# Program order on VectorE, ScalarE and TensorE in parts of a decoder layer, and a second buffer for the weights' side sums

## The chip, the cores and the metric

The kernel runs on one core of a Trainium2 chip. The metric is the device time of one execution in microseconds (us). TensorE multiplies into PSUM; VectorE, ScalarE and GpSimd prepare its operands in SBUF and take its results out of PSUM (GpSimd works on SBUF only); SyncE issues the transfers. The views call these engines PE (PEld is its weight load), DVE, ACT, POOL and SP.

## What is computed

One decoder layer on 1024 tokens of width 1024, in fp32:

```python
x = LN(ALPHA * x + 0.5 * swiglu(x, ffn_w13[0], ffn_w2[0]))      # FFN a
x = LN(ALPHA * x + token_mixer(x))                              # retention and sparse attention
x = LN(ALPHA * x + 0.5 * swiglu(x, ffn_w13[1], ffn_w2[1]))      # FFN b
e = (p @ w_ple) * sigmoid(x @ w_ple_gate)                       # ple
x = LN(ALPHA * x + e)

swiglu(x, w13, w2) = (silu(a) * u) @ w2,   a, u = split(x @ w13)     # inner width 2816
token_mixer(x)     = concat(nsa(x), silu(g) * retention(q, k, v)) @ w_out
retention          : 4 heads of width 128, rotary q and k, chunks of 128 tokens with a decayed state
```

## The kernel before

An fp32 operand is held as two parts, hi and lo. ScalarE makes hi (a rounded copy, L104, L140 or L144), and VectorE or GpSimd makes lo = operand - hi (L105, L141 or L145). A product is three matmuls: hi x hi, lo x hi, hi x lo.

**FFN, first half (up).** It is computed in blocks with seven products in place of eight, by Strassen and Winograd. The 22 tiles of the inner width are numbered f. The first two use plain blocks; from the third tile (f = 2) on, `steps_up` lists (tile, product) steps in program order, 140 of them, and each step is 12 matmuls of 128x512. The operands of a step come from `items_up`: four raw weight blocks wr are loaded for a tile, and side sums of them (s1 to s4) are built by `mix` (L394). A `Stream` holds 8 operands ahead (tiles ch and cl). The results of a tile are put together in `after`: s on ScalarE (L465), t, r, s and h on VectorE (L471 to L482, from PSUM tile Y and the SBUF tile s). They have to be read before TensorE may use those PSUM banks again.

For each pair q of tiles there are two pieces of work in a queue `bg`, one entry of which is emitted after each step: the side sums hq of the result (`pair`, L493 to L502), which are stored to the DRAM tile hd, and the side sums of the second weight (`right_down`). The latter load 1 MB of w2 into the tile w2r, form three differences (L445 to L447) and a fourth (L442) on VectorE in place, and store the whole tile to the DRAM tile td. There is one w2r buffer. Emission is program order, but the order in which an engine runs its instructions is made by a scheduler that may move them; only GpSimd and the places under `self.order(engine)` keep program order.

**FFN, second half (down).** Seven products for each of 11 values of q, in groups of 3, 4 and 4 (`GROUPS`), again with 12 matmuls for each q, operands dr loaded from hd, td and w2. A product of a group is summed over its q in four PSUM banks, and `settle` then adds it to its homes: parts of acc in SBUF on VectorE (L607), or the extra tile u1, whose first use is a copy by ScalarE (L599). acc starts as the residual, 8 loads of 512 KB (L587). The order is `PRODUCTS`: product 0 has the homes c11 in acc and u1; product 5 has u1 alone.

**Retention.** Four heads. For a head, TensorE computes the projections pq and pk (each a PSUM pair of two banks); they are rotated: ScalarE copies halves into sw (L851, L852), and VectorE multiplies by cos straight from PSUM (L853) and adds sw x sin (L856, L857). `ret_head` makes the scores, the states and the output of a head; `weave` spreads these six steps, called side, between the matmuls of the next projection. The list hid, turn and finish is work of the attention's compressed keys that is put in the same gaps. The PSUM tag ps has two pairs. The next weights of a projection are split by ScalarE into wh (L144) when the matmuls that read the old ones are done. Behind the last head comes the projection pg of the gate.

**ple.** The input p is split into pH (ScalarE) and pL (GpSimd, through `split_sb`, L145); the embedding product pe waits for pH, pL and the split weights wh, wl.

Of the kernel before, what the change touches and what calls it, by code (L numbers as in the profile page):

```python
# [10 lines left out]
F32 = mybir.dt.float32  # L11
# [7 lines left out]
P = 128  # L19
# [10 lines left out]
HALF = 512  # L30
NP = NFF // 2
GROUPS = (3, 4, 4)
SLOTS = 8
PRODUCTS = (0, 1, 5, 4, 2, 6, 3)
UORD = [(i, g) for pair in ((4, 2), (5, 1), (6, 0), (3,), (7,)) for g in range(2) for i in pair]


# [86 lines left out]
class Layer:  # L124
# [252 lines left out]
    def items_up(self, j, steps):  # L377

        nc, A = self.nc, self.A
        raw, S = {}, {}  # L380
        left = dict.fromkeys(range(NFF), 0)

        def load(f):
            if f >= NFF or f in raw:
                return
            raw[f] = {}
            for a, b in ((0, 0), (0, 1), (1, 0), (1, 1)):
                t = raw[f][a, b] = self.wr.tile([P, HALF], F32, tag="wr", bufs=self.raws, name=self.nm("wr"))
                nc.sync.dma_start(t, A["w13"][j, f, a, b])

        def mix(name, f, x, y, op):
            e = nc.gpsimd
            t = S[name, f] = self.sm.tile([P, HALF], F32, tag=name, bufs=2 if name == "s2" else 1, name=self.nm(name))
            e.tensor_tensor(t, x, y, op)  # L394
            return t

        def sums(f):
            if (f, "s") not in S:
                S[f, "s"] = True
                r = raw[f]  # L400
                mix("s1", f, r[1, 0], r[1, 1], ALU.add)
                mix("s2", f, S["s1", f], r[0, 0], ALU.subtract)

        for f in (0, 1):
            for a, b in ((0, 0), (1, 0), (0, 1), (1, 1)):
                t = self.wr.tile([P, HALF], F32, tag="wr", bufs=self.raws, name=self.nm("wr"))
                nc.sync.dma_start(t, A["w13"][j, f, a, b])
                yield t, nc.vector
        load(2)
        e = nc.gpsimd  # L410
        for f, p in steps:
            r = raw[f]
            if p == 0:
                yield r[0, 0], e
            elif p == 1:
                yield r[0, 1], e
            elif p == 4:
                sums(f)
                yield S["s1", f], e
            elif p == 5:  # L420
                sums(f)
                yield S["s2", f], e
            elif p == 6:
                yield mix("s3", f, r[0, 0], r[1, 0], ALU.subtract), e
            elif p == 3:
                yield r[1, 1], e
            else:
                yield mix("s4", f, r[0, 1], S["s2", f], ALU.subtract), e
            left[f] += 1
            if left[f] == 3:  # L430
                load(f + 1)

    def right_down(self, j, q):

        nc = self.nc
        raw = self.ub.tile([P, 2, 2, HALF], F32, tag="w2r", bufs=1, name=self.nm("w2r"))
        nc.sync.dma_start(raw, self.A["w2"][j, q])
        b11, b12, b21, b22 = raw[:, 0, 0], raw[:, 0, 1], raw[:, 1, 0], raw[:, 1, 1]
        sub = ALU.subtract

        def final():
            nc.vector.tensor_tensor(b21, b21, b22, sub)  # L442
            nc.sync.dma_start(self.td[j][q], raw.rearrange("p a b n -> p (a b) n"))

        return [lambda: nc.vector.tensor_tensor(b11, b12, b11, sub),  # L445
                lambda: nc.vector.tensor_tensor(b12, b22, b12, sub),
                lambda: nc.vector.tensor_tensor(b22, b22, b11, sub), final]  # L447

    def ffn_up(self, j, B, hooks):

        nc = self.nc
        steps = self.steps_up()
        st = self.stream
        X, YZ, s, t, r, hs, W = {}, {}, {}, {}, {}, {}, {}
        add = ALU.add
        bg = deque()
# [57 lines left out]
        for half, right in enumerate(((B[0], B[1]), (B[6], B[2]))):  # L514
            for f in (0, 1):
# [12 lines left out]
                h = hs[f][:, half]  # L528
# [3 lines left out]
                    x()  # L532
        bg.extend(self.right_down(j, 0))
        pair(0, hs.pop(0), hs.pop(1))
        for f, p in steps:
            if p == 0:
                X[f] = self.one("X")
            if f not in YZ and p > 3:
                YZ[f] = self.two("Y")
            out = X[f] if p < 2 else YZ[f][:, 0] if p in (5, 6, 3) else YZ[f][:, 1]  # L540
            product(out, st.next(), B[p], p in (0, 5, 4), True)
            st.fill()
            after(f, p)
            if bg:
                bg.popleft()()
        while bg:
            bg.popleft()()

    def items_down(self, j):
        nc = self.nc  # L550
        q0 = 0
        todo = []
        for g in GROUPS:
            todo += [(q, p) for p in PRODUCTS for q in range(q0, q0 + g)]
            q0 += g
        srcs = []
        for q, p in todo:
            srcs.append(self.hd[j][q][:, p])
            srcs.append({0: self.A["w2"][j, q][:, 0, 0], 1: self.A["w2"][j, q][:, 1, 0],
                         2: self.A["w2"][j, q][:, 1, 1]}.get(p) if p < 3 else self.td[j][q][:, {3: 2, 4: 0, 5: 3, 6: 1}[p]])  # L560
        srcs = deque(srcs)
        raws = deque()

        def load():
            if srcs:
                t = self.wr.tile([P, HALF], F32, tag="wr", bufs=self.raws, name=self.nm("dr"))
                nc.sync.dma_start(t, srcs.popleft())
                raws.append(t)

        for _ in range(self.raws - 1):  # L570
            load()
        k, n = 0, len(srcs) + len(raws)
        while raws:
            load()
            k += 1
            yield raws.popleft(), nc.vector if k % 4 == 0 or k > n - 16 else nc.gpsimd

    def ffn_down(self, j, ln, residual, pool):

        nc = self.nc  # L580
# [30 lines left out]
        bg = deque()  # L611
        k = 0
        for g, n in enumerate(GROUPS):
            final = g == len(GROUPS) - 1
            for p in PRODUCTS:
                if k % 2 == 0:
                    pair = self.two("py"), self.two("py")
                    banks = [pair[m // 2][:, m % 2] for m in range(4)]
                else:
                    banks = [self.one("py"), self.one("py"), self.one("py"), self.lone("py")]  # L620
                k += 1
                for q in range(n):
                    (hh, hl), (wh, wl) = st.next(), st.next()
                    for m in range(4):
                        ms = slice(m * P, m * P + P)
                        nc.tensor.matmul(banks[m], hh[:, ms], wh, start=q == 0, stop=False)  # L626
                        nc.tensor.matmul(banks[m], hh[:, ms], wl, start=False, stop=False)  # L627
                        nc.tensor.matmul(banks[m], hl[:, ms], wh, start=False, stop=q == n - 1)  # L628
                    st.fill(2)
                    for _ in range({4: 3, 2: 1}.get(p, 4 if q < 1 and p == PRODUCTS[5] else 2)):  # L630
                        if bg:
                            bg.popleft()()
                for m in range(4):
                    settle(p, m, banks[m], final)
                if g == 1 and p in PRODUCTS[:RING]:
                    self.feed.free(1)
                if final and p == 5:
                    for home in (c12, c22, c21):
                        for m in range(4):
                            bg.append(lambda h=home, m=m: nc.vector.tensor_tensor(h(m), h(m), u1(m), add))  # L640
                if final and p == PRODUCTS[4]:
                    while bg:
                        bg.popleft()()
                    norm = [self.ln_fast(m, sums, m) for m in range(4)]
                    bg.extend([x[0] for x in norm])
                    bg.extend(f for x in norm for f in x[1:])
                    bg.extend(lambda m=m: self.to_T(m, 1) for m in range(4))
# [127 lines left out]
    def retention(self, late):  # L775

        nc, tc, A = self.nc, self.tc, self.A
        with ExitStack() as st:
# [44 lines left out]
            weave(v_block(1, None, 0, 4), [parts])  # L823
            parts = blocks(1, pts[1])
            weave(v_block(1, uv1, 4), hid[0])
            side = [parts, nop, *end[0], *hid[1]]
            cst_open = True
            r2 = rt = None
            for h in range(4):
# [15 lines left out]
                for which, pj in (("q", pq), ("k", pk)):  # L845
# [10 lines left out]
                        nc.vector.tensor_tensor(sw, sw, sin[:, s], ALU.mult)  # L856
                        nc.vector.tensor_tensor(dst[:, s], dst[:, s], sw, ALU.add)  # L857
                    qk_t.append(dst)
                side = [nop, nop] + (end[1] if h == 0 else []) + self.ret_head(h, qk_t[0], qk_t[1], v, dec, rc, mh4, r2, rt)
            weave(self.g_block(0, late), side)  # L860
        weave(self.g_block(1, late), [])

# [428 lines left out]
    def ple(self):  # L1291
        nc, tc, A = self.nc, self.tc, self.A
        with ExitStack() as st:
# [31 lines left out]
                    sgs[b, m] = gate(m, u[b])  # L1325
            self.flush_mid(1)
            for kt in range(2):
                self.split_sb(pH[:, kt], pL[:, kt], praw[:, kt])
            self.feed.free(4, pp)
            for m in range(4, NT):  # L1330
                sgs[0, m] = gate(m, u[0])
# [53 lines left out]
    def run(self, ctx):  # L1385
# [35 lines left out]
        with ExitStack() as lst:  # L1421
            late = pool(lst, "late", 1, side="right")
            self.v_r = late.tile([P, NT, 512], F32, name="v_r")
            self.gn = late.tile([P, 2, 512], F32, name="gn")
            self.retention(late)
            np1 = pool(mix, "nsa2", 1)
            self.V = np1.tile([P, NT, 2, 2, P], F32R, name="V")
            self.gate = np1.tile([P, NT, 24], F32, name="gate")
# [117 lines left out]
```

## Time and profile before

| what | us |
|---|---|
| median of 3 runs | 2289.61 (2284.56 to 2297.64) |
| the profiled execution, its own time | 2291.16 |
| its span in the trace | 2288.2 |
| TensorE busy in the span | 2146.6 |
| VectorE, GpSimd, ScalarE busy | 1316.1, 1301.1, 880.9 |

In the trace the parts of the layer follow each other: the up half of FFN a to about 479 us, its down half to about 693, retention to about 1010, sparse attention to about 1440, FFN b to about 2133 (its down half from about 1918), ple to the end. A row of a list of waits gives the instruction that waited, the engine and instruction that ended the wait, the total, the count and the longest one. In a timeline a row is one instruction or several alike, and the brackets give the idle time of the engine before it. In a table of slices the number behind x is the count of instructions and PEclk the share of full speed that the clock of TensorE was granted.

### The profile page before, as it was taken

Reading aid. Unit: us, or ns where it says so; the run is one execution under the profiler, and the core shown is the slowest. Engines: PE = TensorE matmul, PEld = TensorE weight load, DVE = VectorE, ACT = ScalarE, POOL = GpSimd, SP = SyncE. Lnnn points to the kernel's source line nnn. Section 1 sums busy time; section 2 is a strip of 40 time slices with the busy share of each in tenths; the row PEclk is TensorE's granted clock in tenths of the full one; section 3 lists DMA queues with packets and bytes.
Section 4 is the critical chain, followed back from the end, with each engine's and each line's share of the span. In section 5 each row is a group of like instructions: output and inputs, shape, how many; then the busy total and the mean of one; then the engine's idle time right before and its main releaser. Section 6 shows DMA issues by size and latency. Waiting matters only on the chain. (4 is left out here: it accounts for less than half of the span.)

```text
span 2288.2 us, 30883 instructions
## 1 busy us (share of the span) xinstructions
PE 2146.6 (94%) x11112; PEld 1798.2 (79%) x11112; DVE 1316.1 (58%) x2029; ACT 880.9 (38%) x1698; POOL 1301.1 (57%) x1063
## 2 busy tenths in 40 slices
PE   8888999999999889999999999878899999999897
PEld 6666788878877878988788778766788887887797
DVE  7565544446586335522388678866663435657756
ACT  5222233334443332213477677332233333444421
POOL 3766777758853332514356555166677775786334
PEclk9989999999999999999999999999899999999999
DMA  5555432377751221002100002045642326775211
GB/s 187 186 192 207 142 115 93 112 249 222 227 169 33 74 83 37 29 16 79 37 2 20 19 11 78 34 162 195 222 165 92 115 92 228 232 221 166 73 47 74
DMA packets 109881, 271.18 MB, mean 119 GB/s; under 512 B 12576, under 2 KB 12960, under 8 KB 104096
## 3 DMA queue, kind: packets, MB, share of 16 engines
q1 hardware_dynamic: 109728, 269.21, 35.4%
q8 instruction: 87, 1.43, 0.3%
q14 instruction: 66, 0.54, 0.1%
HBM read 197.34 MB, written 71.83 MB: 118 GB/s over the span
## 5 line engine op out<-in xcount | busy, mean ns | idle before, releaser
L105 POOL TENSOR_TENSOR cl<-dr,ch 128x512 fp32r<-128x512 f32 x208 | 283.2, 1385 | 109.7 <-issue 50.1
L105 POOL TENSOR_TENSOR cl<-s,ch 128x512 fp32r<-128x512 f32 x160 | 218.6, 1367 | 194.0 <-ACT ch L104 180.4
L104 ACT ACTIVATE ch<-s 128x512 fp32r<-128x512 f32 x160 | 101.1, 632 | 539.6 <-POOL s L394 393.2
L104 ACT ACTIVATE ch<-dr 128x512 fp32r<-128x512 f32 x308 | 179.0, 624 | 225.9 <-POOL cl L105 107.8
L145 POOL TENSOR_TENSOR wl<-wr,wh 128x1024 fp32r<-128x1024 f32 (+1 forms) x52 | 123.3, 2378 | 249.7 <-ACT wh L144 249.7
L626 PE MATMUL py<-ch,ch 128*128 128x512 f32 x616 | 242.6, 395 | 7.3 <-ACT ch L104 6.9
L627 PE MATMUL py<-cl,ch 128*128 128x512 f32 x616 | 242.9, 394 | 3.8 <-DVE cl L105 3.8
L628 PE MATMUL py<-ch,cl 128*128 128x512 f32 x616 | 242.2, 393 | 0.0
L105 POOL TENSOR_TENSOR cl<-wr,ch 128x512 fp32r<-128x512 f32 x120 | 168.3, 1403 | 106.9 <-ACT ch L104 73.8
L510 PE MATMUL X<-xh,ch 128*128 128x512 f32 x384 | 153.2, 400 | 22.1 <-ACT s L465 16.9
L510 PE MATMUL Y<-xh,ch 128*128 128x512 f32 x352 | 142.7, 417 | 28.3 <-DVE s L477 14.3
L511 PE MATMUL X<-xl,ch 128*128 128x512 f32 x384 | 152.2, 396 | 0.0
L512 PE MATMUL X<-xh,cl 128*128 128x512 f32 x384 | 151.7, 395 | 0.0
L105 DVE TENSOR_TENSOR cl<-dr,ch 128x512 fp32r<-128x512 f32 x100 | 102.4, 1039 | 80.1 <-ACT ch L104 49.4
L607 DVE SCALAR_TENSOR_TENSOR acc<-acc,py 128x512 f32<-128x512 f32 x192 | 120.7, 677 | 48.1 <-PE py L628 39.5
L626 PEld LDWEIGHTS py<-ch,ch 128*128 128x128 f32 x616 | 117.1, 190 | 33.6 <-ACT ch L104 7.7
L511 PE MATMUL Y<-xl,ch 128*128 128x512 f32 x352 | 141.6, 402 | 0.0
L512 PE MATMUL Y<-xh,cl 128*128 128x512 f32 x352 | 141.0, 401 | 0.0
L627 PEld LDWEIGHTS py<-cl,ch 128*128 128x128 f32 x616 | 117.3, 190 | 29.7 <-DVE cl L105 5.5
L1105 POOL TENSOR_SCALAR pr<-pr,ssum,gate 128x640 f32<-128x640 f32 (+7 forms) x128 | 102.1, 806 | 62.3 <-DVE ssum L1102 50.6
L510 PE MATMUL Y<-yh,ch 128*128 128x512 f32 x352 | 137.2, 390 | 0.0
L511 PE MATMUL Y<-yl,ch 128*128 128x512 f32 x352 | 137.0, 389 | 0.0
(290 smaller groups left out, 5919.1 us busy)
## 6 DMA issues: line engine op xcount, KB each, us to landing
wr<-in_w SPq DMA_DIRECT2D x176, 256.0 KB, 3.0
dr<-hd SPq DMA_DIRECT2D x154, 256.0 KB, 3.4
w2r<-in_w SPq DMA_DIRECT2D x22, 1024.0 KB, 5.5
td<-w2r SPq DMA_DIRECT2D x22, 1024.0 KB, 3.9
dr<-td SPq DMA_DIRECT2D x88, 256.0 KB, 3.6
hd<-h SPq DMA_DIRECT2D x66, 256.0 KB, 3.2
hd<-hq SPq DMA_DIRECT2D x22, 768.0 KB, 4.2
dr<-in_w SPq DMA_DIRECT2D x66, 256.0 KB, 3.4
```

The source lines that it names most:

```text
L104: self.ly.nc.scalar.activation(hi, src, AF.Copy)
L105: engine.tensor_tensor(lo, src, f32(hi), ALU.subtract)
L145: self.nc.gpsimd.tensor_tensor(lo, src, f32(hi), ALU.subtract)
L510: nc.tensor.matmul(out, w[0][:, c], b[0][:, kt], start=first and kt == 0, stop=False, skip_group_check=True)
L511: nc.tensor.matmul(out, w[0][:, c], b[1][:, kt], start=False, stop=False, skip_group_check=True)
L512: nc.tensor.matmul(out, w[1][:, c], b[0][:, kt], start=False, stop=end and kt == 3, skip_group_check=True)
L607: nc.vector.scalar_tensor_tensor(a, a, 1.0 if (home, m) in seen else ALPHA, bank, mult, add, accum_out=out)
L626: nc.tensor.matmul(banks[m], hh[:, ms], wh, start=q == 0, stop=False)
L627: nc.tensor.matmul(banks[m], hh[:, ms], wl, start=False, stop=False)
L628: nc.tensor.matmul(banks[m], hl[:, ms], wh, start=False, stop=q == n - 1)
L1105: nc.gpsimd.tensor_scalar(dst, dst, ssum, gate, ALU.mult, ALU.mult)
```

## The change

1. In the first group of the down half, the products come in the order `FIRST`, product 5 ahead of 0; the loads of their operands follow.
2. The side sums (4) and lo parts (7) of the third tile, f = 2, are made on VectorE instead of GpSimd, in each FFN.
3. w2r has two buffers.
4. VectorE runs in program order over the steps of the up half.
5. In retention, TensorE and ScalarE run in program order, and empty steps are put into two of the side lists.
6. In ple, pL is made by VectorE.

```diff
+FIRST = (5, 0, 1, 4, 2, 6, 3)
...
         def mix(name, f, x, y, op):
-            e = nc.gpsimd
+            e = nc.vector if f == 2 else nc.gpsimd
...
         for f, p in steps:
             r = raw[f]
+            e = nc.vector if f == 2 else nc.gpsimd
...
-        raw = self.ub.tile([P, 2, 2, HALF], F32, tag="w2r", bufs=1, name=self.nm("w2r"))
+        raw = self.ub.tile([P, 2, 2, HALF], F32, tag="w2r", bufs=2, name=self.nm("w2r"))
...
-        for f, p in steps:
...
+        with self.order(mybir.EngineType.DVE):
+            for f, p in steps:
...
+                product(out, st.next(), B[p], p in (0, 5, 4), True)
+                st.fill()
+                after(f, p)
+                if bg:
+                    bg.popleft()()
...
-            todo += [(q, p) for p in PRODUCTS for q in range(q0, q0 + g)]
+            todo += [(q, p) for p in (PRODUCTS if q0 else FIRST) for q in range(q0, q0 + g)]
...
-            for p in PRODUCTS:
+            for p in PRODUCTS if g else FIRST:
...
-            side = [parts, nop, *end[0], *hid[1]]
+            side = [parts, nop, nop, nop, *end[0], *hid[1]]
...
-                side = [nop, nop] + (end[1] if h == 0 else []) + self.ret_head(h, qk_t[0], qk_t[1], v, dec, rc, mh4, r2, rt)
+                side = [nop, nop] + ([nop, nop, *end[1]] if h == 0 else []) + self.ret_head(h, qk_t[0], qk_t[1], v, dec, rc, mh4, r2, rt)
...
-                self.split_sb(pH[:, kt], pL[:, kt], praw[:, kt])
+                self.split(pH[:, kt], pL[:, kt], praw[:, kt])
...
-            self.retention(late)
+            with self.order(mybir.EngineType.PE), self.order(mybir.EngineType.Activation):
+                self.retention(late)
```

The order of VectorE near the start of the first up half, before. The number behind a name tells its instances apart: w2r_90, w2r_92 and w2r_159 are those of pairs 0, 1 and 2; s_97, t_111 and r_114 belong to tile 2, s_120 and t_124 to tile 3, counted from 0.

```order
L475 TENSOR_TENSOR r_114_711<-Y_101_647,r_114_711 128x512
L445 TENSOR_TENSOR w2r_92_604<-w2r_92_604 128x512
L446 TENSOR_TENSOR w2r_92_604<-w2r_92_604 128x512
L447 TENSOR_TENSOR w2r_92_604<-w2r_92_604 128x512
L471 TENSOR_TENSOR t_124_759<-Y_121_742,s_120_739 128x512
L442 TENSOR_TENSOR w2r_92_604<-w2r_92_604 128x512
L477 TENSOR_TENSOR s_97_625<-Y_101_647,s_97_625 128x512
L478 SCALAR_TENSOR_TENSOR h_100_644<-h_100_644,s_97_625 128x512
L480 TENSOR_TENSOR t_111_691<-Y_101_647,t_111_691 128x512
L482 SCALAR_TENSOR_TENSOR h_100_644<-h_100_644,r_114_711 128x512
L502 TENSOR_TENSOR hq_158_953<-h_100_644 128x512
L445 TENSOR_TENSOR w2r_159_954<-w2r_159_954 128x512
```

And now, the stretch around the side sums of pair 1 (lines are one or two further down in the file):

```order
L483 SCALAR_TENSOR_TENSOR h_100_646<-h_100_646,r_114_713 128x512
L475 TENSOR_TENSOR r_142_866<-Y_121_744,s_120_741 128x512
L476 TENSOR_TENSOR r_142_866<-Y_121_744,r_142_866 128x512
L446 TENSOR_TENSOR w2r_92_604<-w2r_92_604 128x512
L447 TENSOR_TENSOR w2r_92_604<-w2r_92_604 128x512
L472 TENSOR_TENSOR t_152_911<-Y_149_894,s_148_891 128x512
L448 TENSOR_TENSOR w2r_92_604<-w2r_92_604 128x512
L478 TENSOR_TENSOR s_120_741<-Y_121_744,s_120_741 128x512
L479 SCALAR_TENSOR_TENSOR h_139_848<-h_139_848,s_120_741 128x512
L443 TENSOR_TENSOR w2r_92_604<-w2r_92_604 128x512
L481 TENSOR_TENSOR t_124_761<-Y_121_744,t_124_761 128x512
L483 SCALAR_TENSOR_TENSOR h_139_848<-h_139_848,r_142_866 128x512
```

The sums of pair 1, which stood ahead of tile 2's s and h and were followed at once by those of pair 2, now stand behind r_142 of tile 3, spread between the sums of tiles 3 and 4, and those of pair 2 come after the next pair.

ScalarE in retention, where the second head's pq_1313 is taken out of PSUM, before (wh_1346 is a split of weights into a buffer that the projection pk reads last):

```order
L919 ACTIVATE kz_1327_6948<-pk_1325_6938,rc_5880 128x512
L851 ACTIVATE sw_1349_7077<-pq_1313_6847 64x512
L852 ACTIVATE sw_1349_7077<-pq_1313_6847 64x512
L851 ACTIVATE sw_1350_7081<-pq_1313_6847 64x512
L852 ACTIVATE sw_1350_7081<-pq_1313_6847 64x512
L144 ACTIVATE wh_1346_7070<-wr21_6812 128x1024
L851 ACTIVATE sw_1352_7090<-pk_1324_6931 64x512
L852 ACTIVATE sw_1352_7090<-pk_1324_6931 64x512
L851 ACTIVATE sw_1353_7094<-pk_1324_6931 64x512
```

And now:

```order
L921 ACTIVATE kz_1327_6961<-pk_1325_6951,rc_5887 128x512
L145 ACTIVATE wh_1346_7077<-wr21_6819 128x1024
L853 ACTIVATE sw_1349_7084<-pq_1313_6854 64x512
L854 ACTIVATE sw_1349_7084<-pq_1313_6854 64x512
L853 ACTIVATE sw_1350_7088<-pq_1313_6854 64x512
L854 ACTIVATE sw_1350_7088<-pq_1313_6854 64x512
L853 ACTIVATE sw_1352_7097<-pk_1320_6924 64x512
L854 ACTIVATE sw_1352_7097<-pk_1320_6924 64x512
L853 ACTIVATE sw_1353_7101<-pk_1320_6924 64x512
```

The split wh_1346 stood between the copies of pq and those of pk; it now stands ahead of both.

GpSimd at the start, before (the raw blocks of the third tile are wr_58 to wr_61, those of the next tile start at wr_70; ident is a constant made once):

```order
L105 TENSOR_TENSOR cl_63_408<-wr_58_399,ch_62_407 128x512
L105 TENSOR_TENSOR cl_65_424<-wr_59_401,ch_64_423 128x512
L394 TENSOR_TENSOR s1_66_439<-wr_60_403,wr_61_405 128x512
L394 TENSOR_TENSOR s2_67_441<-s1_66_439,wr_58_399 128x512
L105 TENSOR_TENSOR cl_69_444<-s1_66_439,ch_68_443 128x512
L105 TENSOR_TENSOR cl_75_468<-s2_67_441,ch_74_467 128x512
```

And now:

```order
L106 TENSOR_TENSOR cl_83_539<-wr_70_459,ch_82_538 128x512
L395 TENSOR_TENSOR s1_84_554<-wr_72_463,wr_73_465 128x512
L395 TENSOR_TENSOR s2_85_556<-s1_84_554,wr_70_459 128x512
L106 TENSOR_TENSOR cl_87_559<-s2_85_556,ch_86_558 128x512
masks.py:197 MEMSET ident_63 128x128
masks.py:199 AFFINE_SELECT ident_63<-ident_63 128x128
L106 TENSOR_TENSOR cl_99_643<-s1_84_554,ch_98_642 128x512
```

The operations on wr_58 to wr_61, the third tile, have left GpSimd; its list starts with the fourth.

## Rows read from the trace of the kernel before

**Rows 1.** The profile page: busy time of each engine, its share of the span, and its instructions.

```profile
PE 2146.6 (94%) x11112; PEld 1798.2 (79%) x11112; DVE 1316.1 (58%) x2029; ACT 880.9 (38%) x1698; POOL 1301.1 (57%) x1063
```

**Rows 2.** The table of slices of 50 us: start and end, TensorE, its weight load, VectorE, ScalarE and GpSimd with busy time and count of instructions, granted clock, DMA share and GB/s.

```profile
50.00:100.00 50.00, 40.95 (x168) 32.47 (x167) 29.20 (x29) 14.02 (x25) 35.69 (x28) 0.93 0.53 190
100.00:150.00 50.00, 42.91 (x179) 34.29 (x178) 29.96 (x31) 12.62 (x22) 33.40 (x24) 0.93 0.58 204
150.00:200.00 50.00, 43.77 (x174) 34.74 (x173) 31.36 (x31) 12.46 (x22) 35.75 (x25) 0.90 0.52 184
200.00:250.00 50.00, 42.42 (x171) 34.09 (x170) 26.99 (x30) 11.73 (x20) 27.96 (x20) 0.93 0.51 185
250.00:300.00 50.00, 50.00 (x220) 40.71 (x219) 24.56 (x26) 15.51 (x26) 38.63 (x30) 1.00 0.37 121
...
1500.00:1550.00 50.00, 38.57 (x154) 30.76 (x155) 29.84 (x29) 12.73 (x22) 34.17 (x25) 0.90 0.51 177
1550.00:1600.00 50.00, 41.30 (x180) 32.96 (x178) 28.79 (x32) 12.83 (x23) 34.61 (x26) 1.00 0.54 194
1600.00:1650.00 50.00, 44.09 (x174) 35.03 (x175) 33.23 (x32) 11.84 (x20) 31.68 (x22) 0.91 0.63 223
1650.00:1700.00 50.00, 49.46 (x207) 39.83 (x206) 32.99 (x31) 14.36 (x25) 35.81 (x25) 0.95 0.53 187
```

**Rows 3.** The waits of TensorE over the whole run: instruction that waited, what ended it, us in total, times, the longest.

```profile
PE X L510 <- ACT s L465: 16.9, 2, 9.3
PE Y L510 <- DVE s L477: 14.3, 6, 4.0
PE Y L510 <- DVE t L471: 14.0, 6, 5.3
PE Y L510 <- DVE r L475: 12.2, 6, 6.0
PE py L626 <- ACT ch L104: 6.9, 2, 3.4
...
PE pt L1020 <- DVE ge L1014: 6.6, 2, 3.7
PE pv L751 <- ACT v_r L805: 6.4, 1, 6.4
...
PE pe L752 <- POOL wl L145: 3.7, 1, 3.7
PE pk L914 <- DVE rTk L857: 2.9, 1, 2.9
```

**Rows 4.** The waits of all engines from 60 to 250 us: the row for the w2r loads.

```profile
DVE w2r L445 <- DMA w2r<-in_w: 33.1, 8, 7.2
```

**Rows 5.** The timeline of VectorE from 110 to 156 us: start, duration, line, operation, tiles, and the idle time before it with what ended it.

```profile
116.59 0.69 DVE L445 TENSOR_TENSOR w2r<-w2r 128x512 f32<-128x512 f32 x1 [6.13 <-DMA w2r<-in_w]
...
117.80 1.78 DVE L446 TENSOR_TENSOR w2r<-w2r 128x512 f32<-128x512 f32 x1
...
126.84 0.68 DVE L474 TENSOR_TENSOR r<-Y,s 128x512 f32<-128x512 f32 x1
```

**Rows 6.** The page's DMA issues: tiles, queue, count, KB each, median us from issue to landing.

```profile
w2r<-in_w SPq DMA_DIRECT2D x22, 1024.0 KB, 5.5
```

**Rows 7.** The timelines of GpSimd (first two rows) and ScalarE (last row) at the start.

```profile
32.96 9.62 POOL L105 TENSOR_TENSOR cl<-wr,ch 128x512 fp32r<-128x512 f32 x2 [32.53 <-DVE yl L141]
...
45.15 2.56 POOL L105 TENSOR_TENSOR cl<-s,ch 128x512 fp32r<-128x512 f32 x2
...
61.68 0.63 ACT L104 ACTIVATE ch<-s 128x512 fp32r<-128x512 f32 x1 [3.35 <-POOL s L394]
```

**Rows 8.** Slices of 10 us at the two passages from the up to the down half, columns as in the table of 50 us.

```profile
490.00:500.00 10.00, 6.44 (x28) 4.78 (x26) 4.14 (x5) 4.43 (x8) 8.21 (x7) 1.00 1.00 358
500.00:510.00 10.00, 9.73 (x36) 7.91 (x37) 4.38 (x8) 3.94 (x7) 2.10 (x2) 0.83 1.03 400
...
1930.00:1940.00 10.00, 6.50 (x25) 4.70 (x25) 5.14 (x7) 4.16 (x8) 7.24 (x6) 0.89 0.99 371
1940.00:1950.00 10.00, 10.00 (x36) 7.98 (x35) 3.43 (x6) 3.73 (x6) 2.51 (x3) 0.76 1.00 368
```

**Rows 9.** The timeline of ScalarE from 744 to 758 us, ahead of v_r.

```profile
753.16 1.88 ACT L140 ACTIVATE Xh<-Xr 128x2016 fp32r<-128x2016 f32 x1 [6.78 <-DVE Xr L985]
```

**Rows 10.** The timeline of ScalarE from 846 to 858 us: the first copy of the second head's pq.

```profile
853.14 0.60 ACT L851 ACTIVATE sw<-pq 64x512 f32<-64x512 f32 x1 [2.48 <-PE pkv L926]
```

**Rows 11.** The timelines of ScalarE and VectorE from 922 to 932 us, in order of time: the second head's pk is taken out of PSUM.

```profile
924.15 1.06 ACT L144 ACTIVATE wh<-wr 128x1024 fp32r<-128x1024 f32 x1 [8.45 <-issue]
925.24 0.60 ACT L851 ACTIVATE sw<-pk 64x512 f32<-64x512 f32 x1
...
927.40 0.68 DVE L853 TENSOR_TENSOR rTk<-pk,cos 128x512 f32<-128x512 f32 x1
...
928.12 0.59 ACT L851 ACTIVATE sw<-pk 64x512 f32<-64x512 f32 x1 [1.68 <-DVE rTk L853]
...
930.02 0.68 DVE L853 TENSOR_TENSOR rTk<-pk,cos 128x512 f32<-128x512 f32 x1
```

**Rows 12.** The timeline of GpSimd in ple, from 2160 to 2180 us.

```profile
2168.83 4.68 POOL L145 TENSOR_TENSOR pL<-praw,pH 128x1024 fp32r<-128x1024 f32 x2 [6.39 <-ACT pH L144]
2173.46 2.51 POOL L145 TENSOR_TENSOR wl<-wr,wh 128x512 fp32r<-128x512 f32 x2
```

More of the change, by code (lines that the diff above doesn't have):

```diff
@@ L409, in items_up @@
         load(2)
-        e = nc.gpsimd
         for f, p in steps:
             r = raw[f]
+            e = nc.vector if f == 2 else nc.gpsimd
             if p == 0:
@@ L534, in ffn_up @@
         pair(0, hs.pop(0), hs.pop(1))
-        for f, p in steps:
[L536 to L544, printed above, removed]
+        with self.order(mybir.EngineType.DVE):
+            for f, p in steps:
+                if p == 0:
+                    X[f] = self.one("X")
+                if f not in YZ and p > 3:
+                    YZ[f] = self.two("Y")
+                out = X[f] if p < 2 else YZ[f][:, 0] if p in (5, 6, 3) else YZ[f][:, 1]
+                product(out, st.next(), B[p], p in (0, 5, 4), True)
[3 more added lines that the diff above has]
+                    bg.popleft()()
+            while bg:
                 bg.popleft()()
-        while bg:
-            bg.popleft()()
     def items_down(self, j):
```

## Prediction

> **What bounds the kernel now.** I read the page first. TensorE is busy for 2146.6 of 2288.2 us [rows 1], so time can only come out of its idle stretches and out of the stretches in which it runs slowly. The table of 50 us slices says where they are: the reader should compare the number of matmuls in a slice. An undisturbed slice of the up projection holds 220, that is 0.227 us for one. The four slices from 50 to 250 us hold 168 + 179 + 174 + 171 = 692 instead of 880, and those from 1500 to 1700 us 154 + 180 + 174 + 207 = 715 [rows 2]. At 0.227 us each, the 188 and 165 that are missing are 42.7 and 37.5 us: 80.2 us in two stretches of the same code, one for each FFN. The list of TensorE's waits over the whole run names who is late there: s, t and r on VectorE (14.3 + 14.0 + 12.2 us), and s on ScalarE (16.9 in two waits) [rows 3]. That is 57.4 of the 80.2 us; the rest is the clock, whose granted share is 0.90 to 0.95 in most of these slices and 1.00 where no wait stands [rows 2].
>
> Next, what VectorE does when it is late. From 60 to 250 us it waits eight times, 33.1 us, at L445 for the load of a w2r tile [rows 4]. The timeline shows one: L445 starts at 116.59 after 6.13 us of waiting, three more w2r operations follow, and r, which TensorE needs, starts at 126.84 [rows 5]. One buffer makes load, four operations and store follow each other, and the scheduler had put the pairs' sums one behind the other at the front. Side sums of w2 that are needed only in the second half thus push aside what TensorE needs now; once they are done there is no wait row left (the slice from 250 us has all its 220) [rows 2].
>
> **The change part by part.** The profiled execution took 2291.16 us, 0.07% over the median of 2289.61, so the sum is made against 2291.2.
>
> *VectorE in program order and two w2r homes* belong together. In the new order the sums of pair q+1 come behind the last h of pair q, so four operations per pair, and the load of the next but one is issued when a store is out. A pair is 14 products of 12 matmuls, 14 x 12 x 0.227 = 38.2 us; a w2r load lands in 5.5 us [rows 6]. It is there long before its use. The four operations cost 0.69 us each alone and up to 1.78 beside GpSimd [rows 5], so 2.8 to 7.1 us for each 38.2. VectorE is busy for 24.6 of 50 us in the clean slice [rows 2]; with at most 9.3 more it stays below 34, and by the list of steps t, r and s have two products, 2 x 12 x 0.227 = 5.4 us, before TensorE asks for them. What is behind a waiting instruction now is the rest of VectorE's list in program order, and TensorE behind that; the cover is those 5.4 us. Bounds: nothing is left of the 57.4 - 16.9 = 40.5 us of VectorE's waits and the clock, or half stays. I take nearly all, by the clean slices.
>
> *Third tile on VectorE.* GpSimd begins its list at 32.96 and needs 9.62 us for two lo splits, 2.56 for two later ones. At 61.68 ScalarE has waited 3.35 us for one of its sums, and the s that TensorE wants is queued behind that [rows 7]. This is the first of the two waits that make up the 16.9 us [rows 3]. Eleven operations of this third tile move to VectorE in each FFN, and GpSimd starts with the fourth. VectorE has its own late work there, so some is kept: one late sum of a fourth tile, two GpSimd operations, 2 x 1.28 = 2.6 us, and about 1 of clock, makes 3.5 in each FFN. Both halves: 42.7 - 3.5 = 39 and 37.5 - 3.5 = 34 us gained.
>
> Here a rule speaks against the move. The rows: an operation of VectorE with both inputs in SBUF takes 0.69 us or 1.78, one with an input in PSUM (r from Y) 0.68 [rows 5], and the two lo splits of GpSimd took four times as long while VectorE was full [rows 7]. The Trainium skill (SBUF — State Buffer, "Who interferes with whom") says that such a VectorE operation and a GpSimd operation that reads SBUF share a port pair, held for a whole instruction, and that the other blocks fully. By that rule the eleven operations would not run beside GpSimd's, and the start would gain nothing: 2237 us in place of the 2223 of the sum; the trace agrees with the rule on the price, and that case is rival (c) below.
>
> *Product 5 first in the second half.* TensorE waits 6.9 us in two waits for ch [rows 3] while VectorE waits for acc to settle the first product. From 490 to 510 us there are 28 + 36 = 64 matmuls instead of 88, from 1930 to 1950 us 25 + 36 = 61 [rows 8]: 24 and 27 matmuls, 5.5 and 6.1 us, 3.45 of each the wait and 2 to 2.7 the clock, whose granted share falls to 0.83 and 0.76 behind it (1.00 is 2.4 GHz; part of these slices is at 1.2). Product 5 has one home that ScalarE copies, so acc is needed 3 x 12 = 36 matmuls, 8.2 us, later. The operand loads still queue behind the 4 MB of acc, and the last two td stores come late now: I leave 2.3 us each. 11.6 - 4.6 = 7 gained; bounds 0 and 11.6.
>
> *Retention in program order.* Three waits go. TensorE's 6.4 us for v_r: ScalarE had put the split Xh before it, which starts at 753.16 after 6.78 us of waiting for VectorE [rows 9]; I take 5, since v's tiles then share one PSUM buffer for a while. One of the two waits for ge, 6.6 - 3.7 = 2.9: twelve matmuls now stand before it. The wait of 2.9 for rTk [rows 3] goes, since ScalarE's copies no longer stand apart. Together 10.8. But a new wait comes at each change of head. In the old order ScalarE copies pq out in the middle of the next projection (853.14) [rows 10]; in the new one the split wh stands before it, and wh needs the buffer that the last matmul of pk frees. So pq leaves PSUM only behind the projection, and the next head's pq, which needs those banks, waits. The same chain stands in the trace for pk: wh 1.06, two sw copies of 0.60, rTk 0.68 at 927.40, two sw copies from 928.12, rTk again from 930.02 to 930.70 [rows 11]. From 924.15 that is 6.55 us. Before, this lay beside pg's matmuls; now TensorE has only two empty steps there. Three such changes (to heads 2 and 3 and to the gate): 3 x 6.5 = 19.5, and the clock at 2 each as behind the 3.45 us waits, 6. Bounds: 0, if the rows' waits for other work of VectorE go, and 3 x 9 = 27, with 2.5 of clock each. I take 25.5, because each link of the chain is a row. Net 25.5 - 10.8 = +14.7.
>
> *ple.* pL takes GpSimd 4.68 us for two, and wl, for which TensorE waits 3.7, starts behind it at 2173.46 [rows 3, 12]. pL on VectorE leaves at most 0.7: 3 gained, bounds 0 and 4.
>
> Sum: -39 - 34 - 7 + 14.7 - 3 = -68.3, so 2291.2 - 68.3 = 2223 us.
>
> **Rivals.** (a) The head changes cost nothing, because VectorE and ScalarE get through pq before TensorE asks: 2223 - 25.5 = 2197. For it: at 853 the copies were early. Against it: wh stands before them on ScalarE.
>
> (b) Program order takes back half of the up gain: an operation that waits for TensorE (s, t) now holds those behind it, where the scheduler let a ready one pass. 2223 + 36 = 2259. Against it: the clean slices have the same waits and no loss.
>
> (c) The third tile gains nothing, by the shared port: the two waits, 16.9 us together, stay with 2 us of clock each, 21 instead of 7: 2223 + 14 = 2237. The Trainium skill (SBUF — State Buffer, "Who interferes with whom") would have it so.
>
> Against (c): 22 operations at 1.78 us are 39 us of the shared pair, which the 14 products of two tiles just cover.
>
> (d) Slower: VectorE in program order meets a late w2r load at all 22 pairs. Then the loss is not lifted but spread: 42.7 us over eight waits is 5.3 us a wait, x 22 = 117 in place of 80.2, so 2291 + 37 + 4.7 = 2333. It decides from (80.2 - 4.7) / 22 = 3.4 us a pair on. For it: the load is queued on SyncE behind a store that waits for VectorE itself. Against it: 5.5 us of landing against 38.2.
>
> (e) The change does not do what it says: the waits move to another engine (GpSimd's lo splits of tile four and on) and the up halves keep their time; with +4.7 it gives 2296, no change.
>
> **How the numbers follow.** My forecast 0.51; (a) 0.15; (b) 0.14; (c) 0.13; (d) 0.03; (e) 0.04. Range: from (a) with the 4.6 us left at the boundaries gained too, 2192, to (b) without the 3 us of ple, 2262; outside it lie (d), (e) and the far ends of (a) and (b), under 0.2. A measurement can tell 0.5%, 11.5 us: faster by more than that are the forecast, (a), (b) and (c), 0.93; within it (e), 0.04; slower (d), 0.03.
>
> **What would show it.** In the slices from 50 to 250 us and 1500 to 1700 us 215 to 220 matmuls each, and w2r operations spread over the whole half with hardly a wait for w2r; if the list has w2r waits 20 times, it is (d). No wait of X for s over 3 us; if two of 7 to 9 stay, it is (c). At the boundaries 75 to 85 matmuls in 20 us. In retention three waits of TensorE of 5 to 7 us on rTq L855 or its like, just behind the last matmul of pk; none of them means (a). No wait for wl in ple. The prediction is wrong if the second halves of the up projections, clean now, fall below 215 matmuls a slice.

## The result, and the profile after

The changed kernel takes 2229.26 us (median of 4 runs, 2226.69 to 2231.09); the kernel before, measured beside it, 2287.09. The ratio is 0.974 (95% interval 0.970 to 0.978). The forecast was 2223, 0.3% below, and 2229 lies in its range. The profiled execution took 2231.09, its span is 2229.1. The page again comes first: less TensorE time and nearly the same work on the other engines.

```profile
PE 2129.0 (96%) x11112; PEld 1787.2 (80%) x11112; DVE 1320.7 (59%) x2053; ACT 881.0 (40%) x1698; POOL 1271.3 (57%) x1039
```

The table of slices of 50 us of the changed kernel, with the columns of [rows 2]:

```profile
0.00:50.00 50.00, 44.87 (x189) 36.26 (x190) 42.43 (x69) 31.43 (x51) 2.98 (x6) 1.00 0.58 206
50.00:100.00 50.00, 49.90 (x218) 40.25 (x217) 27.47 (x32) 15.86 (x27) 38.07 (x29) 1.00 0.50 178
100.00:150.00 50.00, 50.00 (x221) 40.92 (x220) 27.14 (x29) 15.24 (x26) 40.51 (x30) 1.00 0.53 184
150.00:200.00 50.00, 50.00 (x220) 40.71 (x219) 28.52 (x30) 15.75 (x27) 39.12 (x29) 1.00 0.42 139
200.00:250.00 50.00, 50.00 (x220) 40.67 (x219) 25.86 (x28) 14.51 (x25) 40.48 (x30) 1.00 0.45 160
...
1500.00:1550.00 50.00, 50.00 (x221) 40.92 (x220) 29.60 (x31) 15.77 (x27) 41.89 (x30) 1.00 0.50 170
```

From 50 to 250 us there are 879 matmuls where [rows 2] have 692, and the clock is granted in full. Every slice from 50 to 400 us and from 1500 to 1850 us has 218 to 221, so the stretches that were clean before stay clean. The waits of TensorE over the whole run, to be read beside [rows 3]:

```profile
PE pq L161 <- DVE rTq L855: 21.8, 3, 9.1
...
PE pg L753 <- DVE rTq L855: 6.2, 1, 6.2
PE py L628 <- ACT ch L105: 6.0, 2, 3.1
...
PE pg L753 <- ACT sg L1312: 2.8, 1, 2.8
...
PE pv L753 <- ACT kc L973: 1.8, 1, 1.8
...
PE X L511 <- ACT s L466: 0.4, 1, 0.4
PE pt L1022 <- DVE ge L1016: 0.3, 1, 0.3
```

The rows for s, t and r on VectorE are gone, the 16.9 us of X are 0.4, and no wait of VectorE for w2r is left. The side sums of a pair now come every 31 to 39 us, the last of the eleven pairs at 432 us of the first up half; before, all eleven were done by 249 us. New at the top stands retention. Where the 59 us between the two traces came from is told by cutting the span at the first matmul or transpose of each stage (up, down, the normalisation ahead of retention, its output projection, and so on). These lengths, taken from the starts of the instructions in the traces, are used for every run below, in us:

| kernel | up a | down a | retention | attention | up b | down b | ple, end |
|---|---|---|---|---|---|---|---|
| before | 468.6 | 222.4 | 285.9 | 465.9 | 464.8 | 223.3 | 152.3 |
| changed | 425.4 | 222.5 | 307.2 | 466.3 | 427.2 | 222.6 | 152.8 |
| no_order | 451.4 | 219.7 | 306.6 | 466.2 | 459.9 | 221.3 | 152.6 |
| one_home | 426.5 | 221.3 | 306.4 | 465.9 | 427.4 | 222.8 | 151.7 |
| third_gpsimd | 435.8 | 221.2 | 306.6 | 465.5 | 437.8 | 222.7 | 153.5 |
| up_only | 436.1 | 224.7 | 283.2 | 465.4 | 437.7 | 224.5 | 150.4 |
| product0_first | 426.0 | 224.1 | 309.5 | 465.9 | 427.3 | 224.6 | 150.7 |
| ret_before | 426.7 | 221.6 | 285.9 | 465.7 | 427.3 | 222.8 | 153.8 |
| ret_pe_only | 425.9 | 221.5 | 286.2 | 462.0 | 426.7 | 221.4 | 153.3 |
| ret_act_only | 426.2 | 221.0 | 302.7 | 466.2 | 427.2 | 220.9 | 153.7 |
| ret_q_early | 426.8 | 221.7 | 287.4 | 463.7 | 427.8 | 221.2 | 155.8 |
| best_pe | 426.0 | 217.2 | 286.5 | 462.2 | 426.7 | 216.7 | 152.3 |
| best_q | 425.5 | 216.4 | 284.2 | 462.4 | 426.7 | 216.4 | 152.3 |
| best_pe_ple | 427.7 | 216.4 | 286.7 | 463.7 | 427.9 | 216.7 | 151.7 |

Stages that no edit touches differ by 2 us and more between kernels (attention 462.0 to 466.3), and ple lies between 150.4 and 155.8, so smaller differences say nothing by themselves. Before to changed: up -43.2 and -37.6, down +0.1 and -0.7, retention +21.3, attention +0.4, ple +0.5.

In retention the waits stand at four changes of head, 9.1, 6.9, 5.8 and 6.2 us. The timelines of ScalarE and VectorE at the second, where TensorE is idle from 822 to 828.9:

```profile
821.67 1.06 ACT L145 ACTIVATE wh<-wr 128x1024 fp32r<-128x1024 f32 x1 [12.95 <-PE pk L162]
822.75 0.59 ACT L853 ACTIVATE sw<-pq 64x512 f32<-64x512 f32 x1
...
826.72 0.59 ACT L853 ACTIVATE sw<-pq 64x512 f32<-64x512 f32 x1 [2.77 <-DVE rTq L855]
```

```profile
826.00 0.69 DVE L855 TENSOR_TENSOR rTq<-pq,cos 128x512 f32<-128x512 f32 x1
...
828.17 0.68 DVE L855 TENSOR_TENSOR rTq<-pq,cos 128x512 f32<-128x512 f32 x1
```

It is the chain of [rows 11], now on pq and with nothing beside it: wh as soon as pk's last matmul is done, copies, rTq, copies, rTq at 828.17 to 828.85, and TensorE starts. The first rTq starts 2 us behind its copies, because VectorE finishes the output of the head before (v_r) until 826.09.

At the first change, where TensorE is idle from 779.7 to 788.8, one more link stands ahead on ScalarE, the activation ge of the attention's compressed keys:

```profile
783.12 0.42 ACT L1015 ACTIVATE ge<-x 126x256 f32<-126x256 f32 x1 [2.79 <-DVE x L1014]
783.45 1.04 ACT L145 ACTIVATE wh<-wr 128x1024 fp32r<-128x1024 f32 x1
784.51 0.59 ACT L853 ACTIVATE sw<-pq 64x512 f32<-64x512 f32 x1
```

At the first passage from up to down, SyncE issues (first two rows) and ScalarE (third row):

```profile
449.85 5.46 SPq L589 DMA_DIRECT2D acc<-in_x  x8
456.35 0.33 SPq L569 DMA_DIRECT2D dr<-td  x1
```

```profile
466.00 4.67 ACT L105 ACTIVATE ch<-dr 128x512 fp32r<-128x512 f32 x7 [9.91 <-DMA dr<-td]
```

An operand load issued behind acc's eight lands some 9.6 us later, and ScalarE stands for 9.91 us; TensorE waits 3 us for that ch. Before, it waited 3.4 us for a ch that stood behind acc [rows 3, 8]. Slices of 10 us at the two passages, columns as in [rows 8]:

```profile
460.00:470.00 10.00, 7.08 (x25) 5.19 (x24) 6.04 (x9) 3.78 (x6) 3.29 (x3) 0.79 1.00 378
470.00:480.00 10.00, 10.00 (x40) 8.13 (x39) 6.20 (x10) 4.21 (x8) 9.04 (x8) 0.87 0.82 244
...
1880.00:1890.00 10.00, 6.96 (x31) 5.44 (x29) 7.74 (x13) 0.60 (x1) 0.72 (x1) 0.96 1.03 406
1890.00:1900.00 10.00, 9.92 (x31) 7.79 (x32) 5.08 (x7) 6.12 (x11) 9.89 (x8) 0.70 0.83 267
```

That is 65 and 62 matmuls in 20 us, against 64 and 61 before: nothing gained, where the prediction wanted 75 to 85.

### The profile page after: what moved, and what is told of

It is laid out like the page before. It is cut to its first block, busy times and chain, and to the rows that moved or that the text cites. A ratio compares the mean times of both kernels' runs of the same rounds, so it can differ in the third digit from the quotient of the medians.

```text
span 2229.1 us, 30878 instructions
## 1 busy us (share of the span) xinstructions
PE 2129.0 (96%) x11112; PEld 1787.2 (80%) x11112; DVE 1320.7 (59%) x2053; ACT 881.0 (40%) x1698; POOL 1271.3 (57%) x1039
## 5 line engine op out<-in xcount | busy, mean ns | idle before, releaser
L106 POOL TENSOR_TENSOR cl<-dr,ch 128x512 fp32r<-128x512 f32 x208 | 282.8, 1383 | 108.7 <-ACT ch L105 52.2
L106 POOL TENSOR_TENSOR cl<-s,ch 128x512 fp32r<-128x512 f32 x152 | 201.8, 1329 | 126.2 <-ACT ch L105 126.2
L106 POOL TENSOR_TENSOR cl<-wr,ch 128x512 fp32r<-128x512 f32 x114 | 161.1, 1414 | 122.0 <-ACT ch L105 119.5
L106 DVE TENSOR_TENSOR cl<-dr,ch 128x512 fp32r<-128x512 f32 x100 | 99.9, 1015 | 87.1 <-ACT ch L105 56.2
L511 PE MATMUL Y<-xh,ch 128*128 128x512 f32 x352 | 137.2, 403 | 0.0
L630 PEld LDWEIGHTS py<-ch,cl 128*128 128x128 f32 x616 | 117.5, 191 | 24.3
```

The costliest lines, as they stand in the source:

```text
L106: engine.tensor_tensor(lo, src, f32(hi), ALU.subtract)
L511: nc.tensor.matmul(out, w[0][:, c], b[0][:, kt], start=first and kt == 0, stop=False, skip_group_check=True)
```

## The experiments

**The second home without the order.** 

```diff
-        with self.order(mybir.EngineType.DVE):
+        if True:
```

> The changed kernel with the scheduler's order on VectorE in the up halves again; two w2r homes and all else stay. My theory: what costs is that the side sums of w2 are pulled to the front, and a second home only lets two of them be loaded at a time. The pairs' sums stand early again, VectorE waits for w2r loads at least 4 times in the first 200 us, and the up halves lose at least half of the 80 us: 2265 to 2310 us. Rival (the second home alone lifts it): no waits, 2224 to 2235 us.

Measured: 2285.75 us, ratio to before 0.9998 (0.9986 to 1.0011). All of the change but this one line comes to nothing in sum: by the stages, the up halves gain 22.1 us and the down halves 4.7, and retention loses 20.7. The line itself is worth 26.0 and 32.7 in the two up halves (no_order against changed). The waits of VectorE for w2r over the whole run, before (first row) and here:

```profile
DVE w2r L445 <- DMA w2r<-in_w: 58.1, 16, 7.2
```

```profile
DVE w2r L446 <- DMA w2r<-in_w: 35.7, 11, 6.9
```

And the waits of TensorE for VectorE here:

```profile
PE Y L511 <- DVE s L478: 21.8, 8, 5.5
PE Y L511 <- DVE t L472: 10.3, 3, 4.8
PE Y L511 <- DVE r L476: 7.1, 2, 4.9
```

The second home takes 22 us off VectorE's waits, but TensorE's are 39.2 in place of 40.5 [rows 3], and the sums stand at the front again: the eleven pairs of the first half are done by 181 us. So it is the place of the sums that costs, and not the waiting for their loads alone. The line also fixes the order of s, t, r and h among themselves; that this is not what helps can be read from the stretches behind the sums, which under the scheduler's order have 219 or 220 matmuls a slice and no such wait (from 250 us before [rows 2], from 200 us here). The theory holds.

**One home with the order.**

```diff
-        raw = self.ub.tile([P, 2, 2, HALF], F32, tag="w2r", bufs=2, name=self.nm("w2r"))
+        raw = self.ub.tile([P, 2, 2, HALF], F32, tag="w2r", bufs=1, name=self.nm("w2r"))
```

> The changed kernel with one w2r home; program order stays. My theory: in program order a pair's load goes out as soon as the pair before is stored, some 25 us before its use, so one home is enough: 2226 to 2234 us, no wait for w2r over 1 us. Rival (the second home is what lifts it, or rival (d) of the prediction, a late load at each pair): 20 waits for w2r and 2250 to 2333 us.

Measured: 2229.69 us, no difference from the changed kernel, and not one wait for w2r. The rival falls: the second home is not needed, and a load at each pair isn't late (rival (d) of the prediction) even with one.

**The third tile back on GpSimd.**

```diff
-            e = nc.vector if f == 2 else nc.gpsimd
+            e = nc.gpsimd
```

(at both places)

> The changed kernel with the third tile's side sums and lo parts on GpSimd again. My theory: the first third-tile product comes late again, one wait of X for s of 7 to 9 us in each FFN and 2 us of clock behind each: 2229 + 14 to 22 = 2243 to 2251 us. Rival (c), by which the shared port makes the move worthless: 2226 to 2234 us.

Measured: 2250.69 us, 21.4 more than the changed kernel, 10.4 and 10.6 of it in the two up halves. TensorE's waits have the old row back:

```profile
PE X L511 <- ACT s L466: 15.3, 2, 9.3
```

So the move is worth 21 us, and rival (c) falls. In the changed kernel GpSimd is busy for 2.98 us of the first 50, and VectorE's 128x512 operations there take 0.68 to 0.69 us each. With the third tile on GpSimd the same operations get slower: one line of VectorE in the first 50 us of the changed kernel, then of this run (four operations, their busy time in us, the mean of one in ns, and the idle time before them):

```profile
L304 DVE TENSOR_TENSOR t<-x,t 128x512 f32<-128x512 f32 x4 | 2.6, 685 | 0.0
```

```profile
L304 DVE TENSOR_TENSOR t<-x,t 128x512 f32<-128x512 f32 x4 | 5.8, 1505 | 0.0
```

A stretch of VectorE in the second up half of the changed kernel, with the third tile's lo parts (L106) among the blocks:

```profile
1455.33 0.69 DVE L106 TENSOR_TENSOR cl<-wr,ch 128x512 fp32r<-128x512 f32 x1
1455.94 0.69 DVE L357 TENSOR_TENSOR d<-d,xl 128x512 f32<-128x512 f32 x1
1456.54 1.29 DVE L356 TENSOR_TENSOR d<-t,xh 128x512 f32<-128x512 f32 x2
```

All have two inputs in SBUF and take 0.69 us or less, not the 1.78 of [rows 5]; GpSimd is idle there, from 1418 to 1469 us. The rule of the Trainium skill (SBUF — State Buffer, "Who interferes with whom"), that such operations and GpSimd's shut each other out, agrees with these rows; what I had drawn from it doesn't. With the third tile on VectorE, GpSimd has nothing to do until the fourth, and there is nobody to share with.

**The order and the homes alone,** on the kernel before (third tile, first product, retention and ple as there).

```diff
-        for f, p in steps:
+        with self.order(mybir.EngineType.DVE):
+            for f, p in steps:
...
-        raw = self.ub.tile([P, 2, 2, HALF], F32, tag="w2r", bufs=1, name=self.nm("w2r"))
+        raw = self.ub.tile([P, 2, 2, HALF], F32, tag="w2r", bufs=2, name=self.nm("w2r"))
```

> The kernel before with two changes alone: program order on VectorE in the up halves and two w2r homes. Third tile, first product, retention and ple as before. My theory: the up halves regain all but the two start waits (16.9 us and 4 of clock): 80.7 - 21 = 60 us less, retention does not get its 21 us, so 2287 - 60 = 2227 us, range 2220 to 2234. Rival (the parts need each other, VectorE in program order falls behind at the start without the third tile): 2240 to 2260 us.

Measured: 2231.2 us. Up falls by 32.5 and 27.1, that is 59.6, as expected. So these two edits alone come within 2 us of the whole change: the gains and losses of the others cancel. The down halves are 2.3 and 1.2 us longer, which is no more than the scatter, but the wait at their start has a new name and is longer:

```profile
PE py L627 <- DVE acc L608: 10.5, 2, 5.6
```

**Product 0 first again.**

```diff
-FIRST = (5, 0, 1, 4, 2, 6, 3)
+FIRST = PRODUCTS
```

> The changed kernel with product 0 first in the down half again. My theory: the edit bought nothing, since the wait moved from VectorE's acc to the operand loads behind acc's 4 MB; 6.3 us are lost at each boundary either way: 2229 within 4 us. Rival (the prediction's term: 3.5 us gained at each): 2234 to 2240 us.

Measured: 2234.03 us, 4.8 more than the changed kernel: just outside my range and at the lower end of the rival's. The down halves are 1.6 and 2.0 longer, and the ratios to before, 0.977 (0.975 to 0.978) and 0.974 (0.970 to 0.978), overlap, so the times alone don't settle it. TensorE's wait does, against the 6.0 of the changed kernel:

```profile
PE py L628 <- DVE acc L609: 10.5, 2, 5.7
```

With the up half in program order, product 0 first waits 5.2 us for acc each time (in up_only too), not 3.4 as before. So product 5 first does gain some 2 us a time, and gives back what the other edit costs there; my expectation of no effect was wrong. In no_order, where that cost is absent, the down halves are 2.7 and 2.0 shorter than before. VectorE's own waits for acc show that acc comes later with the order (4.1 us each time before, 6.7 and 7.4 in up_only); why was not tried. That the last pairs' stores now stand there is a guess.

**Retention as before.**

```diff
-            with self.order(mybir.EngineType.PE), self.order(mybir.EngineType.Activation):
-                self.retention(late)
+            self.retention(late)
...
-            side = [parts, nop, nop, nop, *end[0], *hid[1]]
+            side = [parts, nop, *end[0], *hid[1]]
```

(and the two empty steps of head 0 out)

> The changed kernel with the retention as it was (scheduler's order on all engines there, no added empty steps). My theory: program order costs retention 21 us net by the trace; without it 2229 - 21 = 2208 us (2203 to 2213), no wait of pq for rTq over 2 us, and the old waits for v_r (6.4) and ge (6.6) back. Rival (the up halves' shift moves these waits anyway): 2225 to 2233 us.

Measured: 2209.48 us, 20 less; retention takes its old 285.9, with its old waits. Its edit costs 20 us in the changed kernel.

**TensorE's order alone, and ScalarE's alone.**

```diff
-            with self.order(mybir.EngineType.PE), self.order(mybir.EngineType.Activation):
+            with self.order(mybir.EngineType.PE):
```

> The changed kernel with program order in the retention on TensorE alone; ScalarE is scheduled. My theory: the head-change waits come from ScalarE's place of wh ahead of the copies of pq; a scheduler that places the copies first takes them away, 28 us of waits and 5 of clock, while the waits for ge stay small: 2229 - 20 to 33 = 2196 to 2209 us. Rival (TensorE's program order makes them: it asks for pq's banks with nothing else to do): waits of 5 to 9 us stay, 2222 to 2232 us.

```diff
-            with self.order(mybir.EngineType.PE), self.order(mybir.EngineType.Activation):
+            with self.order(mybir.EngineType.Activation):
```

> The changed kernel with program order in the retention on ScalarE alone; TensorE is scheduled. My theory: ScalarE's order makes the waits, so three or four waits of TensorE of 5 to 9 us at the changes of head stay, and the time is 2222 to 2234 us. Rival (TensorE's order makes them): they go, 2200 to 2212 us.

Measured: 2208.14 and 2225.14 us. The rows of TensorE's waits with its own order alone, from 640 to 960 us, and then with ScalarE's alone, over the run:

```profile
PE pq L161 <- DVE rTq L855: 8.1, 1, 8.1
PE pv L753 <- ACT v_r L807: 6.9, 1, 6.9
```

```profile
PE pq L161 <- DVE rTq L855: 16.8, 3, 6.9
...
PE pt L1022 <- DVE ge L1016: 6.6, 2, 4.2
PE pg L753 <- DVE rTq L855: 6.2, 1, 6.2
```

ScalarE's order makes the three later waits. The first, 8 to 9 us, stays with TensorE's order alone, which I had not expected. With ScalarE's order alone TensorE loses as much there, in two pieces: 4.2 for ge and then 4.1 for rTq. Before, it lost 6.1 at this place (3.7 for ge, 0.5 for another operation of ScalarE, 1.8 for rTq). So most of the first wait is an old loss under another name. TensorE's order alone is no better than the old retention: it loses the waits for ge and rTk and takes that one for them.

**Copies of pq between the projections,** with both orders kept.

```diff
                 def qk():
                     yield 16
                     yield from self.proj_T(pq)
+                    if not cst_open:
+                        qk_t.append(rotate("q", pq))
                     nonlocal pk
...
-                    r2, rt = pool("r2", 2), pool("rt", 4)
+                    r2, rt = pool("r2", 2), pool("rt", 6)
```

(shortened; rotate is the body of the loop over q and k, unchanged, and rt gets six buffers)

> The changed kernel with program order kept on TensorE and ScalarE in the retention, but the rotation of pq written between the projections pq and pk for heads 1 to 3 (six rt buffers instead of four). My theory: then wh no longer stands before the copies, the waits at the changes to heads 2, 3 and the gate (6.9 + 5.8 + 6.2) go and the first one (9.1) stays: 2229 - 19 - 5 = 2205 us (2200 to 2213). Rival (what makes pq late is VectorE's output of the head before, not ScalarE's order): at least two waits over 3 us stay, 2217 to 2230 us.

Measured: 2208.53 us, 20.7 less. One wait of this kind is left, at the change that the edit leaves alone:

```profile
PE pq L161 <- DVE rTq L842: 9.0, 1, 9.0
```

So, with ret_pe_only, the place of wh ahead of the copies is what made the other three.

**acc's loads one by one.** 

```diff
-        for m in range(8):
-            nc.sync.dma_start(acc[:, m, :], residual(m))
+        late = deque(range(8))
...
                     st.fill(2)
+                    if late:
+                        i = late.popleft()
+                        nc.sync.dma_start(acc[:, i, :], residual(i))
```

(on three kernels; best_pe, with TensorE's order alone in retention, is compared with ret_pe_only)

> The changed kernel with program order in the retention on TensorE alone (2208 us measured), and the eight loads of acc issued one by one behind the operand loads of the first eight (product, q) steps of the down half instead of in a block ahead of them. My theory: what TensorE waits for at the boundary is an operand load behind acc's 4 MB; spread out, the waits of 2.9 and 3.1 us and the clock behind them, 6.3 us at each boundary, go: 2208 - 10 to 13 = 2195 to 2198 us. Rival (the stores of the last pairs or the sum of the bytes fill the queues, not acc's place): the waits stay or move to acc, 2204 to 2212 us.

> The same spreading of acc's loads, on the kernel with the rotation of pq between the projections and program order on TensorE and ScalarE (2208.5 us measured). My theory: 2196 to 2199 us, no different from the one with TensorE's order alone, since both keep one wait of 8 to 9 us at the first change of head. Rival as there: 2204 to 2212 us.

> The first of these kernels with pL on GpSimd again, as before the change. My theory: the edit in ple moved a wait of 2.9 us from wl to the sigmoid's place on ScalarE and gained nothing: within 3 us of the first, either way. Rival (the prediction's term): 3 us slower.

Measured: 2199.73, 2198.97 and 2198.37 us; the first has the ratio 0.962 (0.960 to 0.964) to before. TensorE has no wait of this kind left at the boundary. Slices of 10 us of the first, where the changed kernel has 65 matmuls in 20 us:

```profile
460.00:470.00 10.00, 10.00 (x46) 8.29 (x45) 5.56 (x10) 4.59 (x8) 6.52 (x5) 1.00 1.04 397
470.00:480.00 10.00, 10.00 (x46) 8.28 (x45) 8.97 (x15) 5.83 (x10) 8.22 (x7) 1.00 0.88 311
```

Against ret_pe_only down gains 4.3 and 4.7 us, 8.4 in the medians, a little under the 10 to 13 expected: acc's place in the queue was the cause, since the bytes are the same. The three differ by less than they scatter, so pL's engine makes no difference, and each of them beats both kernels: some 30 us, 1.4%, under the changed one.

## Why the prediction was right, and what was off in it

- **Program order against early side sums** (40.5 us of VectorE's waits and the clock): right, and shown; one line carries it. That the two w2r homes belong with it was wrong: one does as well, and two without the order leave TensorE's waits as they were.
- **Third tile**: right, but mis-sized. I kept 3.5 us in each FFN for VectorE's own late work; 0.4 of wait is left. Up gained 80.8, not 73.
- **Boundaries**, 7 us gained: this step failed. Of the two things in it, acc needed later and operand loads behind acc, the second was put at 2.3 us and measured as all that is lost there: 65 and 62 matmuls in 20 us are 23 and 26 too few, 5.2 and 5.9 us, as much as before. The wait changed its name from acc to dr. And the order of the up half lengthens the wait for acc by some 2 us each time (10.5 us in two in up_only, 6.9 before), which was not in the sum.
- **Retention**, +14.7: right in mechanism, +21.3 in size. The chain of 6.55 us was measured as 6.9, 5.8 and 6.2. What failed is the count of three: the first change has one too, 9.1 us, where 6.1 were lost before. The 5 us that I took for v_r were 3.2 (1.4 for v_r and 1.8 for kc are left of 6.4), and TensorE's order added one wait of 2.7 at the start of the stage (pc for acc). All idle time of TensorE in this stage rose by 16.2 us; the other 5 of the 21.3 go with the clock (granted share 0.93 over the stage, 0.96 before), a little under the 6 that I had allowed.
- **ple**, -3: wrong. The wait for wl went, but the scheduler now puts ScalarE's split of weights ahead of a sigmoid. The timeline of ScalarE there:

```profile
2106.83 0.63 ACT L145 ACTIVATE wh<-wr 128x512 fp32r<-128x512 f32 x1 [7.38 <-DMA wr<-in_wpl]
...
2109.61 0.64 ACT L1312 ACTIVATE sg<-pg 128x256 f32<-128x256 f32 x2
```

ScalarE waits 7.38 us for a load, and TensorE 2.8 for the sigmoid behind it. best_pe_ple, with pL back on GpSimd, is no slower: the wait for the sigmoid is gone, and that for wl is back:

```profile
PE pe L756 <- POOL wl L146: 2.9, 1, 2.9
```

In the two traces the change took 59.1 us off and not 68.3, because 7.8 more from the up halves stood against 6.6 more from retention, 6.4 less at the boundaries, 3.5 less in ple, and 0.4 in the attention, which is scatter. So it is in part luck that 2229 lies 6 us from 2223: the misses run both ways, and the sum was made from an execution of the kernel before that took 2291.2 us, 4 more than the 2287.09 measured beside the result.

## What to carry to other kernels

Work that is needed late and depends on a load should not be free to move ahead on an engine that others wait for: an order, not another buffer, was worth 60 us here. An order on a second engine is to be read row by row for what it puts ahead of the instruction that frees a buffer: one split of weights ahead of four copies, at three changes of head, cost 20 us. And a wait that is named after one transfer may have another right behind it in the same queue: issue what is needed later, later.

## What the runs showed of the hardware

VectorE's 128x512 operations with both inputs in SBUF took 0.69 us where GpSimd was idle and up to 1.8 beside it: 0.685 and 1.505 on average for the same line with the third tile on VectorE and on GpSimd. Those with an input in PSUM did not slow down: in the first up half of the kernel before, the 97 that read X or Y while GpSimd worked took at most 0.69 us each, and the 125 with both inputs in SBUF 1.19 on average.

Loads in one queue landed in the order of issue at the passage: the eight of acc, 512 KB each, from 456.29 to 465.23 us, some 1.28 apart, and the operand load of 256 KB behind them at 465.90. It took some 9.6 us, where the page gives 3.6 as the median of the same loads.

```profile
dr<-td SPq DMA_DIRECT2D x88, 256.0 KB, 3.6
```
